# The last four heads of a two-layer decoder trunk: y loaded in place, one chain of fill work, a strictly ordered tail, and weight low parts on VectorE

## The chip, the cores and the metric

The kernel runs on one core of one Trainium2 chip. The metric is the device time in microseconds of one execution; smaller is better. Engine names in the profile are PE (TensorE, matrix products), DVE (VectorE), ACT (ScalarE), POOL (GpSimd) and SP (SyncE, which here only issues transfers). PEld is the weight load of TensorE.

## The reference

One sequence of 1024 positions and width 1024 goes through two residual layers and a final norm.

```
h = rms_norm(x, norm_g[0]);  x = x + lru_mixer(h, ...)          # layer 0: gated linear recurrence
h = rms_norm(x, norm_g[1])                                      # layer 1: forgetting attention, 16 heads of 64
u = h @ fox_w_in                                                # q, k, v, gate (1024 each) and 16 forget logits
cum = cumsum(log_sigmoid(f_logit + b_f))                        # over positions
logits = (q . k) / 8 + cum[query] - cum[key], masked causally
o = softmax(logits) @ v;   y = o * silu(gate)
x = x + y @ fox_w_out
return rms_norm(x, final_g)
```

Everything is float32. The change lies in the second layer, from its twelfth head (counted from 0) to the end: in the gate projection of the last pair of heads, in `y @ fox_w_out`, and in the final norm.

## The kernel before, in words

**Precision.** A matrix product is made of three: each float32 operand is split into a high part (rounded to the type float32r) and a low part (the rest), and high by high, low by high and high by low are accumulated in PSUM. So each weight block costs a cast on ScalarE (`to_hi`, line 75) and a subtraction (`to_lo`, line 86). `split_weights` (L88) loads a block of up to 4 x 128 columns to a tile `wf` (3 buffers), writes `wh` and `wl` (4 buffers each); `weights` (L99) does that for one column block of a weight matrix, with the subtraction on GpSimd unless `lo_eng` says otherwise. `gemm_steps` (L105) issues the three products (L111, L112, L113) for one tile of 128 x 512 and gives control back after every two blocks: one step is six products.

**The attention.** Heads come in pairs. Per head and per half c of the positions there are two streams of work: `maxima(hd, c)` (L631) makes the logits tile S of four query blocks, takes their maxima on VectorE (L659) and their exponentials on ScalarE (L662); `weigh(hd, c)` (L701) makes the transposed logits ST (L723, L724), their exponentials p (L729, L732), masks the diagonal on GpSimd (L737), splits p to `ph` and `pl` on VectorE (L81, L86), and accumulates p times v in O (L757, L758). `scale` (L696) multiplies the gate `sg` by the reciprocal sums on GpSimd (L699), `gated` (L766) multiplies the pair's result by it on GpSimd (L772) and gives y, 128 rows (a pair) by 512 positions.

**Order.** `run(order, ...)` (L786) reads a string: a digit takes a step of that stream of attention work, a dot takes a step of `fill`, other products that are to keep TensorE busy. The orders of heads 12 to 14 hold 16 dots each, the first order of head 15 holds 4, and its last two quarters of positions hold 18 and 11. A planner then puts the instructions of each engine in a fixed order, by program order and by its own estimate of when each is ready; `tc.issue_after(ins)` tells it that what the block issues on the engine of `ins` stands behind `ins` there. Each engine works through its own list strictly in order.

**What the fill is.** For an even head: `kq_units(pair + 1)` (16 steps), the next pair's keys and queries; for an odd head `g_units(pair + 1)` (8 steps), its gate. Both read `hT`, the normed input, whose 2 x 8 high and low tiles hold all 16 buffers of the tags `hh` and `hl`. In head 12 both are chained (24 steps), 16 at its dots, 8 at its end, so that `hT` is read for the last time there. From head 13 the fill is `partial` (L811, 48 steps): 16 tiles (db, c) of the output product over the first six pairs, added on VectorE to the residual x (L822), which is read from and written back to DRAM (`x1d`, L819 and L823). Its first 36 steps stand at the dots of heads 13, 14 and 15, the other 12 in the first quarter, whose last 6 dots are empty.

**y.** The y of pairs 0 to 5 goes to DRAM (`y1d`). `load_y` (L805) brings each of the 12 tiles back to a tile of the tag `xp` (3 buffers, shared with the x of `partial`), and `split_y` (L798) writes its high part on ScalarE (L75, `yhh<-y`) and its low part on VectorE (L86, `yhl<-y`) to tiles of the tags `hh` and `hl`, which come free as `hT` is no longer read. The y of pairs 6 and 7 is split directly.

**The end.** `turned(c, q)` (L827) handles a quarter of the positions: it loads the residual in four tiles (L832), and for each of two blocks b and two halves h of the width it transposes the residual onto PSUM (L850), adds the output product of pairs 6 and 7 (L854 to L856; their weights come from `late`, L883), and squares on ScalarE with a row sum (L860). For c = 0 the tile is multiplied by the norm's weight (L862) and the root is taken later for all four blocks (`root_mean`, L872; L956). For c = 1 both halves stay in PSUM until the root is known, and one VectorE instruction each (L867) multiplies by root and weight:

```
for pt, hs in zip(pts, halves):
    nc.vector.scalar_tensor_tensor(res[:, b, hs], pt, r, grow[:, hs], ALU.mult, ALU.mult)
    nc.sync.dma_start(out[4 + 2 * q + b, :, hs], res[:, b, hs])
```

The steps of `turned(0, 0)` and `turned(0, 1)` (16) are the fill of the last quarter and its rest; `turned(1, 0)` and `turned(1, 1)` follow with no order of their own.

## Time and profile before

| what | value |
|---|---|
| median of 3 runs | 1155.97 us (1154.35 to 1156.48) |
| the profiled execution | 1159.8 us |
| its span, from the first to the last instruction | 1157.9 us |
| mean granted TensorE clock of the span | 0.994 |
| PE busy | 1131.8 us (98% of the span) |
| DVE busy | 818.3 us (71%) |
| ACT busy | 590.7 us (51%) |
| POOL busy | 311.0 us (27%) |

A row of the timeline gives the start in us, the duration in us, the engine, the line of the kernel, the operation, the tile written and the tiles read, the shape, and in brackets how long the engine had been idle and what ended that. A trailing xN says that N instructions were merged in the row. A matmul's duration includes its passage through the array, and successive ones overlap; the distance between two starts is what one costs. A window's row gives for each engine the busy time in the stretch, the number of instructions, the granted TensorE clock as a share of full speed, the share of the DMA engines that were busy and the GB/s that they moved. The chain of work that ended last is followed back from the last instruction, and its pieces are shown in order of time.

### The profile page before, as it was taken

The page shows a single profiled execution, that of the slowest core. Times are in us where ns is not written, and L with a number is a line of the kernel's source. Part 1 is how long each engine was busy: PE and PEld are TensorE (multiplying, and loading weights), DVE is VectorE, ACT ScalarE, POOL GpSimd, SP SyncE. Part 2 cuts the span into 40 slices and gives each one's busy share as a digit, 9 for nine tenths or more (in the row PEclk, how much of TensorE's full clock was granted, in tenths as well). Part 3 has the DMA queues.
Part 4 walks back from the last instruction along what each step waited for, and adds up shares of the span by engine and source line. Part 5 has one row for each costly group of instructions (what it writes and reads, how often), then busy time and mean ns, then how long its engine had stood idle before and what let it go on. Part 6 is the DMA issues. An engine that isn't in the chain of part 4 may idle for free.

```text
span 1157.9 us, 15580 instructions
## 1 busy us (share of the span) xinstructions
PE 1131.8 (98%) x5565; PEld 944.8 (82%) x5565; DVE 818.3 (71%) x1294; ACT 590.7 (51%) x1009; POOL 311.0 (27%) x305
## 2 busy tenths in 40 slices
PE   9999999999999999999999999999999999999897
PEld 7787888888888887978888988889888898777685
DVE  7589766677566889556877757777577775577754
ACT  8388345345544656454554545545454454445323
POOL 1212212112021103342332333323333233141310
PEclk9999999999999999999999999999999999999898
DMA  6111111111111124351343323433234331646244
GB/s 211 51 41 50 51 51 55 42 50 41 51 59 37 55 73 151 98 142 38 92 120 92 92 64 92 120 92 83 65 92 110 92 84 60 182 138 202 80 159 182
DMA packets 60221, 105.41 MB, mean 91 GB/s; under 512 B 8744, under 2 KB 23720, under 8 KB 60144
## 3 DMA queue, kind: packets, MB, share of 16 engines
q1 hardware_dynamic: 60144, 104.42, 31.9%
q8 instruction: 44, 0.72, 0.3%
q14 instruction: 33, 0.27, 0.1%
HBM read 63.30 MB, written 15.93 MB: 68 GB/s over the span
## 4 chain that ended last, share of the span: by engine, by line
PE 47%; DVE 5%; ACT 2%; DMA 2%; issue 1%; POOL 1%; DVEq 0%; SPq 0%; ACTq 0%; POOLq 0%
PE gps L111 6%; PE gps L112 6%; PE gps L113 6%; PE O L758 3%; PE ST L723 3%; PE S L655 2%; PE S L654 2%; PE ST L724 2%; PE O L757 2%; PE vps L519 2%; PE vps L517 2%; PE vps L518 2%; DVE pl L86 2%; PE ops L112 1%; PE ops L113 1%
## 5 line engine op out<-in xcount | busy, mean ns | idle before, releaser
L86 POOL TENSOR_TENSOR wl<-wf,wh 128x512 fp32r<-128x512 f32 (+2 forms) x130 | 189.0, 1458 | 504.7 <-ACT wh L75 428.6
L111 PE MATMUL gps<-hh,wh 128*128 128x512 f32 x576 | 226.8, 394 | 1.1 <-DVE qkl L555 0.7
L113 PE MATMUL gps<-hl,wh 128*128 128x512 f32 x576 | 226.7, 394 | 0.0
L112 PE MATMUL gps<-hh,wl 128*128 128x512 f32 x576 | 226.7, 394 | 0.0
L75 ACT CAST wh<-wf 128x512 fp32r<-128x512 f32 (+2 forms) x156 | 94.0, 607 | 140.1 <-PE gps L113 43.1
L662 ACT ACTIVATE S<-S,st 128x128 f32<-128x128 f32 (+7 forms) x128 | 91.4, 714 | 114.0 <-DVE st L659 112.9
L113 PEld LDWEIGHTS gps<-hl,wh 128*128 128x128 f32 x576 | 108.3, 188 | 24.3 <-issue 0.2
L111 PEld LDWEIGHTS gps<-hh,wh 128*128 128x128 f32 x576 | 108.4, 188 | 22.6 <-DVE qkl L555 1.1
L112 PEld LDWEIGHTS gps<-hh,wl 128*128 128x128 f32 x576 | 108.5, 188 | 21.6 <-issue 0.5
L86 DVE TENSOR_TENSOR pl<-p,ph 128x512 fp32r<-128x512 f32 (+2 forms) x130 | 121.7, 953 | 2.3
L81 DVE CAST ph<-p 128x512 fp32r<-128x512 f32 (+2 forms) x130 | 79.2, 619 | 57.0 <-ACT p L729 30.2
L737 POOL TENSOR_SCALAR_AFFINE_SELECT p<-p 128x128 f32<-128x128 f32 (+1 forms) x128 | 47.5, 388 | 201.6 <-ACT p L729 98.1
L659 DVE CUSTOM_DVE_ANT_0 S<-S,mask 128x128 f32<-128x128 f32 (+7 forms) x128 | 96.6, 758 | 7.1 <-PE S L655 6.2
L351 DVE TENSOR_TENSOR x<-x,ops 128x512 f32<-128x512 f32 x80 | 54.0, 681 | 50.7 <-PE ops L113 50.6
L111 PE MATMUL ups<-hh,wh 128*128 128x512 f32 x192 | 76.3, 397 | 2.6 <-DVE us L261 1.9
L113 PE MATMUL ups<-hl,wh 128*128 128x512 f32 x192 | 75.9, 395 | 0.2
L112 PE MATMUL ups<-hh,wl 128*128 128x512 f32 x192 | 75.7, 394 | 0.3 <-POOL wl L86 0.3
L758 PE MATMUL O<-pl,v 128*128 128x512 f32 (+1 forms) x198 | 67.1, 348 | 7.8 <-DVE pl L86 7.8
L729 ACT ACTIVATE p<-ST 128x512 f32<-128x512 f32 (+1 forms) x68 | 53.0, 785 | 42.4 <-PE ST L724 35.5
L518 PE MATMUL vps<-wh,hl 128*128 128x256 f32 (+1 forms) x256 | 72.7, 285 | 0.0
L517 PE MATMUL vps<-wh,hh 128*128 128x256 f32 (+1 forms) x256 | 72.6, 285 | 0.0
L519 PE MATMUL vps<-wl,hh 128*128 128x256 f32 (+1 forms) x256 | 72.4, 284 | 0.0
(192 smaller groups left out, 2517.7 us busy)
## 6 DMA issues: line engine op xcount, KB each, us to landing
wf<-in_w SPq DMA_DIRECT2D x100, 256.0 KB
wf<-in_wo SPq DMA_DIRECT2D x64, 128.0 KB
T<-qkh SPq DMA_DIRECT2D x28, 256.0 KB
U<-qkh SPq DMA_DIRECT2D x28, 256.0 KB
x<-in_xt SPq DMA_DIRECT2D x16, 256.0 KB
x1d<-x SPq DMA_DIRECT2D x16, 256.0 KB
wf<-in_wv SPq DMA_DIRECT2D x16, 256.0 KB
xp<-x1d SPq DMA_DIRECT2D x16, 256.0 KB
```

Source lines behind the costliest of these rows:

```text
L75: nc.scalar.copy(hi, src)
L81: eng.tensor_copy(hi, src)
L86: return eng.tensor_tensor(lo, src, f32(hi), ALU.subtract)
L111: nc.tensor.matmul(o, wh, xh[:, cs], start=i == 0, stop=False)
L112: nc.tensor.matmul(o, wl, xh[:, cs], start=False, stop=False)
L113: nc.tensor.matmul(o, wh, xl[:, cs], start=False, stop=i == len(pairs) - 1)
L517: nc.tensor.matmul(pt, xh, wh, start=k == 0, stop=False)
L518: nc.tensor.matmul(pt, xl, wh, start=False, stop=False)
L519: nc.tensor.matmul(pt, xh, wl, start=False, stop=k == KT - 1)
L659: nc.vector.tensor_tensor_reduce(S[:, :n], S[:, :n], mask[:, SEQ - n :], -1.0, -NEG, ALU.add, ALU.min, accum_out=m)
L662: seen[0] = nc.scalar.activation(S[:, :n], S[:, :n], AF.Exp, bias=f32(m), scale=-1.0, accum_out=sums[:, i : i + 1])
L758: nc.tensor.matmul(o, v, pl[:, jj, : ns[jj]], start=False, stop=j == nj - 1)
```

## The change

1. `partial` asks for its weights' low parts on VectorE (`lo_eng=nc.vector`) instead of GpSimd.
2. `load_y(c)` brings the six tiles of y straight to the tiles that will hold their low parts; `split_loaded(c)` later casts the high part from there and subtracts in place. The tag `xp` is no longer used for y.
3. One chain is the fill from head 12 to the end: keys and queries of pair 7 (16 steps), the first half of its gate (4), `load_y(0)`, the second half (4), `load_y(1)`, `split_loaded(0)`, two tiles of `partial` with c = 0, `split_loaded(1)`, the other fourteen, `turned(0, 0)`, `turned(0, 1)`. It is 88 steps long; 17 are taken in head 12, 16 each in heads 13 and 14, 4 in the first order of head 15, 18 and 11 in the quarters, 6 at the end. So 7 of the gate's 8 steps go from head 12 to head 13, and no dot is empty.
4. For c = 1, each first half is multiplied by the norm's weight as soon as it is there, the second between the sum and the root; the root is then applied on ScalarE to the first half and on VectorE to the second. The residuals of c = 1 are requested ahead of the first half's output. Each step of `turned(1, 0)` and `turned(1, 1)` is put behind the last product of the step before.
5. The norm's weight (`grow`) is requested one quarter earlier, and two dots of the first quarter's order are moved by a place.

```diff
@@ -485,9 +485,8 @@
...
-        def project(cb_i, use, hs=(0, 1)):
-
-            w = list(weights(w1[cb_i]))
+        def project(w, use, hs=(0, 1)):
+
@@ -530,10 +529,11 @@
...
         kq = {}
+        wo = {}
         sgs = {}
...
         yos = {}
-        y1 = [[], []]
+        y1 = [{}, {}]
@@ -554,7 +554,7 @@
...
-                yield from project(is_k * 8 + pair, use, hs)
+                yield from project(list(weights(w1[is_k * 8 + pair])), use, hs)
@@ -615,16 +615,21 @@
...
         forget(1)
-        def g_units(pair):
-
-            sg = sgs[pair] = at.tile([P, SEQ], F32, tag="sg", name="sg1")
+        gw = [None]
+
+        def g_units(pair, hs=(0, 1)):
+
+            if hs[0] == 0:
+                sgs[pair] = at.tile([P, SEQ], F32, tag="sg", name="sg1")
+                gw[0] = list(weights(w1[16 + pair]))
+            sg = sgs[pair]
...
-            yield from project(16 + pair, use)
+            yield from project(gw[0], use, hs)
@@ -773,7 +778,7 @@
...
             if hd >= 13:
-                split_y(c, yo, nc.vector, sub)
+                split_y(c, pair, yo, sub)
             else:
@@ -795,47 +800,59 @@
...
-        def split_y(c, y, eng, sub=slice(0, HALF)):
-            if sub.start == 0:
-                y1[c].append(tuple(hpool.tile([P, HALF], F32R, tag=t, name="y" + t) for t in ("hh", "hl")))
-            yh, yl = (z[:, sub] for z in y1[c][-1])
+        def pair_of_y(c, pair):
+            y1[c][pair] = tuple(hpool.tile([P, HALF], F32R, tag=t, name="y" + t) for t in ("hh", "hl"))
+            return y1[c][pair]
+
+        def split_y(c, pair, y, sub=slice(0, HALF)):
+            yh, yl = (z[:, sub] for z in (pair_of_y(c, pair) if sub.start == 0 else y1[c][pair]))
             to_hi(yh, y, nc.scalar)
-            to_lo(yl, y, yh, eng)
-
-        def load_y(c, pairs):
-            for pair in pairs:
-                y = at.tile([P, HALF], F32, tag="xp", name="y", bufs=3)
-                nc.sync.dma_start(y, y1d[c, pair])
-                split_y(c, y, nc.vector)
-
-        def partial():
-
-
-            ws = {}
-            for db, c in [(0, 0), (1, 0), (0, 1), (1, 1)] + [(db, c) for db in range(2, KT) for c in range(2)]:
-                if db not in ws:
-                    ws[db] = list(weights(wo1[db, :, :6]))
+            to_lo(yl, y, yh, nc.vector)
+
+        def load_y(c):
+            for pair in range(6):
+                nc.sync.dma_start(f32(pair_of_y(c, pair)[1]), y1d[c, pair])
+            yield from ()
+
+        def split_loaded(c):
+            for pair in range(6):
+                yh, yl = y1[c][pair]
+                to_hi(yh, f32(yl), nc.scalar)
+                to_lo(yl, f32(yl), yh, nc.vector)
+            yield from ()
+
+        def partial(todo):
+
+
+            for db, c in todo:
+                if db not in wo:
+                    wo[db] = list(weights(wo1[db, :, :6], lo_eng=nc.vector))
                 x = at.tile([P, HALF], F32, tag="xp", name="xp", bufs=3)
...
                 pt = ps.tile([P, HALF], F32, tag="g", name="ops1")
-                yield from gemm_steps(pt, zip(ws[db], y1[c]))
+                yield from gemm_steps(pt, zip(wo[db], [y1[c][pair] for pair in range(6)]))
                 nc.vector.tensor_tensor(x, x, pt, ALU.add)
...
-        def turned(c, q):
-
-
+        left, turn = {}, [None]
+
+        def residual(c, q):
             xs = [wpool.tile([P, 2, 256], F32, tag=("wh", "wl")[q], name="x1") for d in range(4)]
...
                 nc.sync.dma_start(x, x1d[c, :, 2 * d : 2 * d + 2, q * 256 : (q + 1) * 256])
+            return xs
+
+        def turned(c, q):
+
+
+            xs = left.pop((c, q), None) or residual(c, q)
...
                 ss = ssq[c][:, 4 * q + 2 * b : 4 * q + 2 * b + 2]
-                pts = []
                 for h, hs in enumerate(halves):
@@ -843,7 +860,6 @@
...
                         pt = ps.tile([P, HALF], F32, tag="gO"[c * q], name="turn")
-                    pts.append(pt)
@@ -853,27 +869,30 @@
...
                         nc.tensor.matmul(pt, yl, wh, start=False, stop=False)
-                        nc.tensor.matmul(pt, yh, wl, start=False, stop=k == 1)
+                        turn[0] = nc.tensor.matmul(pt, yh, wl, start=False, stop=k == 1)
                         if k == 0:
...
                     nc.scalar.activation(sq, pt, AF.Square, accum_out=ss[:, h : h + 1])
-                    if c == 0:
+                    if c == 0 or h == 0:
                         nc.vector.tensor_tensor(res[:, b, hs], pt, grow[:, hs], ALU.mult)
+                        yield
+                if c == 1:
+                    r = root_mean(ss, lambda: nc.vector.tensor_tensor(res[:, b, hs], pt, grow[:, hs], ALU.mult))
+                    nc.scalar.activation(res[:, b, halves[0]], res[:, b, halves[0]], AF.Copy, scale=r)
+                    nc.vector.tensor_scalar(res[:, b, hs], res[:, b, hs], r, None, ALU.mult)
+                    for hs in halves:
+                        nc.sync.dma_start(out[4 + 2 * q + b, :, hs], res[:, b, hs])
                     yield
-                if c == 1:
-                    r = root_mean(ss)
-                    for pt, hs in zip(pts, halves):
-                        nc.vector.scalar_tensor_tensor(res[:, b, hs], pt, r, grow[:, hs], ALU.mult, ALU.mult)
-                        nc.sync.dma_start(out[4 + 2 * q + b, :, hs], res[:, b, hs])
             if c == 0:
...
-        def root_mean(ss):
+        def root_mean(ss, between=lambda: None):
...
             nc.vector.tensor_tensor(r, r, ss[:, :, 1], ALU.add)
+            between()
             nc.scalar.activation(r, r, AF.Sqrt, bias=epst, scale=1.0 / SEQ)
@@ -906,16 +925,25 @@
...
             if hd % 2 == 0:
-                if hd < 14:
+                if hd < 12:
                     fill = kq_units(pair + 1)
+                elif hd == 12:
+                    rest = [(db, c) for db in range(2, KT) for c in range(2)]
+                    fill = chain(
+                        kq_units(7),
+                        g_units(7, (0,)),
+                        load_y(0),
+                        g_units(7, (1,)),
+                        load_y(1),
+                        split_loaded(0),
+                        partial([(0, 0), (1, 0)]),
+                        split_loaded(1),
+                        partial([(0, 1), (1, 1)] + rest),
+                        turned(0, 0),
+                        turned(0, 1),
+                    )
             elif pair < 6:
                 fill = g_units(pair + 1)
-            if hd == 12:
-                fill = chain(fill, g_units(7))
-            if hd == 13:
-                load_y(0, range(3, 6))
-                load_y(1, range(6))
-                fill = partial()
             first, second = ORDERS[hd < 15 and (hd > 11 or hd % 2 == 0)]
@@ -926,12 +954,11 @@
...
             gated(hd, 1)
-            if hd == 12:
-
-                take(fill, 4)
-                load_y(0, range(3))
-            if hd < 13:
+            if hd < 12:
                 drain(fill)
+            elif hd == 12:
+
+                take(fill, 1)
             if hd % 4 == 3 and hd < 12:
@@ -939,24 +966,28 @@
...
         gated(15, 0)
-        run("0.....0...0.......0...", weigh(15, 1, quarters[0]), fill=fill)
-        drain(fill)
-        scale(15, slice(HALF, SEQ))
-        gated(15, 1, quarters[0])
         grow = at.tile([P, SEQ], F32, tag="sg", name="grow")
...
         first = []
-        fill = chain(turned(0, 0), turned(0, 1))
+        run("0.....0....0......0...", weigh(15, 1, quarters[0]), fill=fill)
+        scale(15, slice(HALF, SEQ))
+        gated(15, 1, quarters[0])
         run("0..0....0.0..0..", weigh(15, 1, quarters[1]), fill=fill)
...
+
+        for q in range(2):
+            left[1, q] = residual(1, q)
         r = root_mean(ssq[0])
...
             nc.sync.dma_start(out[i], o)
-        for q in range(2):
-            drain(turned(1, q))
+        tail = chain(turned(1, 0), turned(1, 1))
+        while turn[0] is not None:
+            with tc.issue_after(turn[0].ins):
+                if next(tail, tail) is tail:
+                    break
```

## The prediction, made before the changed kernel was run

> **What bounds the kernel now.** I read the page's busy shares first, then the stretch from head 12 to the end cut at the places where TensorE pauses, then who TensorE waited for.
>
> ```profile
> PE 1131.8 (98%) x5565; PEld 944.8 (82%) x5565; DVE 818.3 (71%) x1294; ACT 590.7 (51%) x1009; POOL 311.0 (27%) x305
> core 0: us, PE busy (x) PEld busy (x) DVE busy (x) ACT busy (x) POOL busy (x), PEclk, DMA share, GB/s
> 975.00:1020.00 45.00, 42.55 (x193) 34.19 (x192) 28.24 (x49) 20.41 (x38) 7.13 (x12) 1.00 0.54 147
> 1020.00:1070.00 50.00, 49.47 (x234) 40.35 (x233) 36.04 (x69) 24.27 (x50) 15.21 (x18) 1.00 0.58 171
> 1070.00:1084.00 14.00, 10.17 (x37) 8.06 (x37) 11.88 (x13) 4.10 (x9) 7.01 (x9) 0.76 0.31 98
> 1084.00:1113.70 29.70, 29.64 (x149) 24.69 (x148) 18.15 (x31) 9.16 (x17) 8.54 (x11) 1.00 0.36 116
> 1113.70:1137.50 23.80, 23.40 (x141) 20.00 (x140) 11.86 (x22) 9.10 (x25) 2.11 (x4) 1.00 0.46 143
> 1137.50:1157.90 20.40, 11.76 (x60) 8.88 (x58) 9.68 (x21) 7.42 (x22) 0.00 (x0) 0.83 0.54 207
> PE O L758 <- DVE pl L86: 5.1, 2, 3.8
> PE turn L850 <- ACT sq L860: 2.5, 1, 2.5
> PE ST L723 <- ACT S L662: 1.6, 2, 1.2
> PE turn L850 <- DMA x<-x1d: 0.4, 1, 0.4
> ```
>
> TensorE sets the time: it is busy for 98% of the span, and the change takes no product away and adds none. So it can only win back time in which TensorE pauses or runs at less than full clock. Subtracting the busy column from each stretch gives the pauses: 2.45 us before 1020, 0.53 to 1070, 3.83 in the 14 us after it, 0.06, 0.40, and 8.64 at the end. The last four rows (wait in us, how often, the longest) name them: two waits for `pl`, one for a square, two for an exponential, one for the residual's transfer. The row 1070 to 1084 shows a second loss, a clock of 0.76. The next rows show that place on three engines (DVE, POOL, PE), and two rows from a quiet place for comparison.
>
> ```profile
> 1069.56 7.00 DVE L86 TENSOR_TENSOR pl<-p,ph 128x1024 fp32r<-128x1024 f32 x1
> 1069.46 2.39 POOL L699 TENSOR_TENSOR sg<-sg,recb 64x1024 f32<-64x1024 f32 x1 [14.22 <-DMA recb<-recd]
> 1071.80 0.55 POOL L737 TENSOR_SCALAR_AFFINE_SELECT p<-p 128x128 f32<-128x128 f32 x2
> 1072.30 3.18 POOL L86 TENSOR_TENSOR wl<-wf,wh 128x512 fp32r<-128x512 f32 x3
> 1076.62 0.80 PE L758 MATMUL O<-pl,v 128*128 128x512 f32 x1 [3.83 <-DVE pl L86]
> 1077.21 0.63 PE L757 MATMUL O<-ph,v 128*128 128x512 f32 x1
> ...
> 1082.33 0.50 PE L113 MATMUL ops<-yhl,wh 128*128 128x512 f32 x1
> 1005.48 0.39 PE L112 MATMUL ops<-yhh,wl 128*128 128x512 f32 x1
> 1005.71 0.40 PE L113 MATMUL ops<-yhl,wh 128*128 128x512 f32 x1
> 1066.60 1.22 DVE L86 TENSOR_TENSOR pl<-p,ph 128x1024 fp32r<-128x1024 f32 x1
> ```
>
> The subtraction that gives `pl` takes 7.00 us where the same one just before took 1.22. During it GpSimd ran without a break for 2.39 + 0.55 + 3.18, and VectorE's instruction ended about one us after GpSimd's last. I read it as VectorE standing still while GpSimd works. The Trainium skill, page "SBUF — State Buffer", section "Who interferes with whom", gives the reason: a VectorE instruction with two SBUF inputs shares a read path with GpSimd, and whoever starts first holds it for the whole instruction; the rows agree. After 3.83 us of idleness TensorE comes back slow: from 1077.21 to 1082.33 there are twelve distances between starts, 5.12 / 12 = 0.43 us each, against 0.23 at 1005.48. That is 12 x 0.20 = 2.4 us. This place costs 3.83 + 2.4 = 6.2 us.
>
> **Low parts on VectorE.** 8 weight tiles with two pieces each, 16 subtractions, leave GpSimd for VectorE. Their rows between 995 and 1115 (14 of 16), VectorE's price for the same two shapes (here of y), and what stays on GpSimd:
>
> ```profile
> L86 POOL TENSOR_TENSOR wl<-wf,wh 128x512 fp32r<-128x512 f32 x7 | 9.2, 1315 | 16.8 <-ACT wh L75 16.5 <-POOL sg L699 0.4
> L86 POOL TENSOR_TENSOR wl<-wf,wh 128x256 fp32r<-128x256 f32 x7 | 6.2, 885 | 12.3 <-ACT wh L75 12.0 <-DMA xp<-x1d 0.2
> L86 DVE TENSOR_TENSOR yhl<-y,yhh 128x512 fp32r<-128x512 f32 x12 | 8.0, 687 | 8.2 <-ACT yhh L75 7.9 <-PE gps L112 0.3
> L86 DVE TENSOR_TENSOR yhl<-yo,yhh 128x256 fp32r<-128x256 f32 x2 | 0.8, 416 | 0.0
> L772 POOL TENSOR_TENSOR yo<-yo,sg 128x512 f32<-128x512 f32 x3 | 4.1, 1370 | 7.0 <-DVE yo L763 7.0
> ```
>
> VectorE gets 8 x 0.687 + 8 x 0.416 = 8.8 us more. Its rows from 975 to 1113.7 add up to 28.24 + 36.04 + 11.88 + 18.15 = 94.3 of 138.7 us, 68%; with 8.8 more 74%. The sum is covered by TensorE's own work, the queue is not: behind each subtraction stand VectorE's casts and subtractions for `ph` and `pl`, which TensorE awaits at O, and the subtraction itself waits for ScalarE's cast, which waits for the weight's transfer. GpSimd loses 8 x 1.315 + 8 x 0.885 = 17.6 us and with it most of its power to hold VectorE up. At 1069.56, 3.18 of GpSimd's 6.1 us go away, so `pl` comes 3.18 earlier, TensorE idles 0.65 us, and I take it that the clock then stays up, as it did in the rows of 975 to 1020 with a wait of 1.2: gain 3.18 + 2.4 = 5.6. Bounds: 6.2 if the rest closes too; nothing, if VectorE is by then so late that the pause returns. The new load costs 0 where it falls into the free 26%, and at most two waits like the one of 1.2, 2.4; I take 1.0, nearer to the free share. The other side of the skill's rule speaks against the edit: the moved subtractions have two SBUF inputs, so GpSimd's remaining 2.39 and 1.37 us instructions can hold them up as well; by it one or two in 16 would last about a us longer, which the 1.0 contains.
>
> **y in place.** The 12 transfers, 12 casts and 12 subtractions all stay. They no longer pass through the three buffers `xp`, but their room is free only once TensorE has read `hT` for the last time, half by half.
>
> ```profile
> L75 ACT CAST yhh<-y 128x512 fp32r<-128x512 f32 x12 | 7.2, 619 | 8.9 <-DMA y<-y1d 8.9
> 992.81 8.69 SPq L808 DMA_DIRECT2D y<-y1d  x6
> ```
>
> Now ScalarE waits 8.9 us in all for these transfers, six of which take SP 8.69 us because each waits for a buffer; the transfers of weights stand behind them in SP's queue. With 7 of the gate's 8 steps moved into head 13, four steps of fill (24 products at 0.23, 5.5 us) plus attention work stand between `load_y` and its use, and the same for the second half: I cost the transfers at nothing, hidden by those steps; were they not, TensorE would wait about one transfer queue, 8.69 less 5.5, some 3. But six casts and six subtractions now come in one piece: 6 x 0.619 = 3.7 us on ScalarE and 6 x 0.687 = 4.1 on VectorE, with exponentials and `pl` behind them. The wait of 1.2 for an exponential and the smaller one for `pl` (5.1 - 3.8 = 1.3) are of that kind already. I take back 1.0 of the 2.45; bounds a gain of 2.45 and a loss of 3.
>
> **The strict tail.**
>
> ```profile
> 1146.87 2.43 ACT sq L860 x8
> 1149.35 0.65 PE L850 MATMUL turn<-ident,x 128*128 128x128 f32 x4 [2.51 <-ACT sq L860]
> 1150.94 0.41 PE turn L855
> 1151.35 0.44 PE turn L856
> 1152.53 0.17 DVE ssq L876
> 1153.05 0.18 DVE ssq L878
> 1153.32 1.41 DVE L867 SCALAR_TENSOR_TENSOR res<-turn,ssq,grow 128x512 f32<-128x512 f32 x2
> 1139.28 2.74 DVE L956 TENSOR_SCALAR res<-res,ssq 128x1024 f32<-128x1024 f32 x4
> ```
>
> The planner mixed the tiles of c = 1: four were squared in one go, and the last tile waited 2.51 us for a bank. The eight tiles of c = 1 have eight banks by their tags (two each of g and O, two pairs of S), so in strict order no tile has to wait for another of its kind: 2.5 gained. Bounds: 2.9, with the slow clock of the last two products (0.41 and 0.44 against 0.23), and 1.0, if strict order makes TensorE wait for a residual or for a bank of c = 0. After the last square the old way was sum, root, inverse, 1.41: 2.2 us from 1152.53 to 1154.73. The new one is sum 0.17, product 0.7, inverse 0.18, then ScalarE's scaling (a cast of that size took 0.62) beside VectorE's (2.74 / 8 = 0.34): about 1.8 with hand-overs, but the first half's transfer, until now 0.7 us ahead of the second's, starts later than before. I take 0; bounds a gain of 0.4 and a loss of 0.4.
>
> **One chain.** TensorE's sum is unchanged and no step is lost. But `partial` now ends one dot into the last quarter, and `turned(0, 0)` needs its last buffers and its last residual.
>
> ```profile
> 1113.84 0.24 PE ops L112
> 1114.60 4.49 DMA x<-x1d
> 1119.14 0.44 PE turn L850 x2
> ```
>
> From the chain of waits: the residual took 4.49 us after the last product of `partial`, covered until now by the last quarter's attention; TensorE lost only the 0.40 seen above. One of that quarter's four pairs of key blocks (8 products of half the width, half of 0.23 each, 0.9 us) may now stand ahead of it, so I take a loss of 0.7; bounds 0 and 2.7 (4.49 less a first tile of `turned`, whose residual is there: 0.44 for the transposes and six products at 0.23, 1.8).
>
> **Sum.** -5.6 + 1.0 - 1.0 - 2.5 + 0.7 = -7.4 us. The profiled execution took 1159.8 (span 1157.9, the other 1.9 outside it), so it would take 1152.4. It lies 3.8 above the median of 1155.97; I carry the gain over: 1148.6.
>
> **The rivals.** *VectorE's queue becomes the bound (slower).* A moved subtraction waits at the head of VectorE's queue for a weight that is late, `pl` waits behind it, and TensorE pauses long enough to lose its clock. For it: the idle columns above show that GpSimd sat 16.5 and 12.0 us for ScalarE's cast, a wait that VectorE inherits where it gets there early. Against: ScalarE's queue stands still in the same wait already. Price: 6.2 per case, the place at 1069. It decides from the second case on: -7.4 + 2 x 6.2 = +5.0, 1161. Chance 0.13.
>
> *The pause returns elsewhere.* TensorE's pauses in heads 13 to 15 stay as long as before, since the planner does not know that GpSimd holds VectorE and its new order makes a new collision; only the tail's 2.5 holds, less 0.7 and 1.0: 1155.2. For it: 2.39 us of GpSimd's scaling remain at each head. Against: only one of these pauses was over 1.3 us. Chance 0.19. By the Trainium skill ("TensorE: Matmul & The Clock Gate", "HAM oscillation — how this bites in real kernels") an idle time of about 3.4 us costs the clock; here 3.83 did and 1.2 did not, which agrees.
>
> *All pauses go.* 3.83 + 2.4 + 2.45 + 0.53 + 2.9 = 12.1: 1143.9. For it: the fill has no empty dots. Against: the bursts of casts. Chance 0.10.
>
> *The forecast*, between 1145 and 1153: 0.58.
>
> **The numbers.** A measurement of this kernel tells about 0.2%, 2.3 us, from no change. Below 1153.7 lie the forecast, the last rival and a third of the second: 0.58 + 0.10 + 0.06 = 0.74, less 0.02 for the forecast's upper edge, 0.72. Within 2.3 us lie the rest of the second and that edge, 0.15; above, 0.13. The range leaves out the slower rival (0.13) and the best few cases: 1143.5 to 1157.5.
>
> **What would show it.** In the changed profile no `wl` on GpSimd from head 13 on; no `pl` above 4.5 us; the clock 1.00 from 975 to 1137; the largest wait of TensorE before the tail under 2 us; no wait of a transpose for a square; the span's last product 2 to 3 us nearer to the one that ends `partial`. Wrong: a wait of TensorE over 3 us followed by a clock below 0.9, a VectorE row for `wl` that stands idle for ScalarE's cast with `pl` behind it, or casts of y that wait for transfers.

## The result and the profile after: slower by 0.9%

The changed kernel takes 1166.31 us (median, 1165.29 to 1167.63); the kernel before took 1156.11 beside it. The ratio is 1.0089, with a 95% interval of 1.0076 to 1.0103. The forecast was 1148.6 and a range up to 1157.5. The profiled execution of the changed kernel took 1165.29 (span 1163.6).

First the page's busy row, then the stretch from head 12 to the end cut where TensorE pauses now (columns as in the prediction), then who TensorE waited for there.

```profile
PE 1134.5 (98%) x5565; PEld 946.6 (81%) x5565; DVE 826.0 (71%) x1314; ACT 593.7 (51%) x1013; POOL 293.6 (25%) x289
```

```profile
975.00:1000.00 25.00, 25.00 (x119) 20.89 (x118) 14.96 (x27) 9.64 (x18) 2.05 (x6) 1.00 0.56 145
1000.00:1030.00 30.00, 24.58 (x95) 18.21 (x94) 26.46 (x50) 18.30 (x37) 6.31 (x8) 0.83 0.51 135
1030.00:1062.00 32.00, 32.00 (x151) 26.55 (x150) 20.52 (x41) 12.34 (x26) 2.86 (x5) 1.00 0.42 140
1062.00:1070.00 8.00, 5.25 (x17) 3.95 (x16) 5.10 (x7) 4.25 (x7) 3.08 (x3) 0.79 0.56 170
1070.00:1113.00 43.00, 43.00 (x215) 36.13 (x214) 30.19 (x55) 13.70 (x28) 7.72 (x12) 1.00 0.40 126
1113.00:1142.00 29.00, 28.86 (x162) 24.06 (x161) 13.33 (x24) 10.90 (x28) 1.84 (x3) 1.00 0.48 154
1142.00:1163.60 21.60, 11.18 (x57) 8.32 (x56) 9.98 (x24) 8.36 (x22) 0.00 (x0) 0.96 0.51 195
```

```profile
PE turn L866 <- DVE res L878: 4.5, 2, 2.6
PE ST L728 <- ACT p L734: 3.1, 2, 2.7
PE O L763 <- DVE pl L86: 2.6, 3, 0.9
PE S L659 <- ACT S L667: 1.3, 1, 1.3
```

TensorE runs without a gap from 975 to 1000, 1030 to 1062 and 1070 to 1113. It loses at three places: 1000 to 1030 (5.42 us idle and a clock of 0.83), 1062 to 1070 (2.75 idle, 0.79), and the tail.

To put one number on a stretch I add up, over its products, by how much the distance to the next start exceeds the distance at full speed (0.23 us for 512 columns, 0.12 for 256, as the rows of quiet places show). This counts idle time and slow products alike, and the span less all such losses is about 1117 us in the kernel before (1157.9 - 40.6) and after (1163.6 - 46.6; 40.6 and 46.6 are the sums of their rows), so losses account for the difference. In us, by trace:

| kernel | to 975 | place 1, 1000-1035 | place 2, 1040-1085 | 1085-1125 | tail, from 1125 | span |
|---|---|---|---|---|---|---|
| before | 22.5 | 3.4 | 8.3 | 1.4 | 5.0 | 1157.9 |
| before, second profile (e4) | 23.4 | 2.8 | 4.0 | 1.9 | 5.7 | 1155.0 |
| after | 21.9 | 11.9 | 4.7 | 0.6 | 7.5 | 1163.6 |
| e2: after, two tiles in the tail | 21.6 | 11.1 | 3.8 | 1.5 | 2.5 | 1157.4 |
| e3: before, low parts on VectorE | 21.7 | 2.4 | 1.6 | 1.5 | 5.3 | 1149.6 |
| e7: e3, strict order, two tiles | 24.5 | 3.2 | 1.5 | 1.6 | 1.8 | 1149.6 |
| e8: e2, y through `xp` | 23.0 | 9.7 | 7.1 | 0.2 | 3.2 | 1162.2 |
| e9: e2, gate in head 12 | 22.7 | 7.5 | 1.5 | 2.2 | 2.0 | 1152.8 |
| e11: e9, a late piece moved | 21.6 | 3.1 | 0.6 | 3.0 | 1.5 | 1146.7 |
| e13: e9, y through `xp` | 22.7 | 3.5 | 1.5 | 2.5 | 1.7 | 1148.7 |

Each row is one execution. Up to 975, where the edits do not reach, the rows differ by up to 2.9 us; the profile of e9 is the slowest of its ten runs (1154.62), that of e11 the fastest of its ten (1148.42); e8 loses about 2 us more between 1035 and 1040, outside the columns.

So place 2 loses 3.6 us less than in the profile that the prediction used, but 0.7 more than in the second one, while place 1 loses 8.5 and the tail 2.5 more. Place 1, read on five engines (timeline of the changed kernel):

```profile
992.53 4.89 SPq L814 DMA_DIRECT2D yhl<-y1d  x5
1004.28 0.39 PE L113 MATMUL gps<-hl,wh 128*128 128x512 f32 x1
1012.73 0.47 SPq L695 DMA_DIRECT2D recb<-recd  x1
1016.25 2.60 POOL L704 TENSOR_TENSOR sg<-sg,recb 64x1024 f32<-64x1024 f32 x1 [1.24 <-DMA recb<-recd]
1019.52 1.28 POOL L777 TENSOR_TENSOR yo<-yo,sg 128x512 f32<-128x512 f32 x1
1020.84 0.62 ACT L75 CAST yhh<-yo 128x512 fp32r<-128x512 f32 x1 [2.63 <-POOL yo L777]
1021.36 3.22 ACT L75 CAST yhh<-yhl 128x512 fp32r<-128x512 f32 x6
1022.87 0.63 PE L111 MATMUL ops<-yhh,wh 128*128 128x512 f32 x1
```

The last product of the gate starts at 1004.28 and the first of `ops` at 1022.87: for 18.6 us TensorE has no fill at all, only attention work with its short waits (the `pl` and S rows above). The y transfers of the first half were issued by 997.4. Their six casts run only at 1021.36, directly behind the cast of `yo`, which is the split of pair 6 and waits for the whole chain of that head's sums: `recb`, GpSimd's scaling 2.60, its gating 1.28. On ScalarE's list the six casts stand behind that split. The second half's transfers were issued only from 1021.26 to 1025.9, and their casts waited 0.99 and 0.46 us for them (at 1027.93 and 1029.01).

Place 2 and the tail in the same timeline:

```profile
1055.62 1.65 ACT L75 CAST woh<-wf 128x512 fp32r<-128x512 f32 x3
1064.21 0.62 ACT L75 CAST woh<-wf 128x512 fp32r<-128x512 f32 x1 [6.94 <-DMA wf<-in_wo]
1064.74 1.94 ACT L734 ACTIVATE p<-ST 128x1024 f32<-128x1024 f32 x2
1065.81 0.50 PE L728 MATMUL ST<-U,T 128*128 128x512 f32 x1 [2.75 <-ACT p L734]
1141.48 2.74 DVE L984 TENSOR_SCALAR res<-res,ssq 128x1024 f32<-128x1024 f32 x4
1146.15 0.66 PE L866 MATMUL turn<-ident,x 128*128 128x128 f32 x4 [2.65 <-DVE res L878]
1155.59 0.66 PE L866 MATMUL turn<-ident,x 128*128 128x128 f32 x4 [1.83 <-DVE res L878]
```

At place 2 a late weight's cast stands in ScalarE's queue 6.94 us for its transfer, two exponentials stand behind it, and TensorE waits 2.75 for them. In the tail the second half of block b = 1 waits twice for the reader of its first half. Both halves lie in one tile, `two_banks`.

### The profile page after: what moved, and what is told of

It is laid out like the page before. It is cut to its first block, busy times and chain, and to the rows that moved or that the text cites. A ratio compares the mean times of both kernels' runs of the same rounds, so it can differ in the third digit from the quotient of the medians.

```text
span 1163.6 us, 15563 instructions
## 1 busy us (share of the span) xinstructions
PE 1134.5 (98%) x5565; PEld 946.6 (81%) x5565; DVE 826.0 (71%) x1314; ACT 593.7 (51%) x1013; POOL 293.6 (25%) x289
## 4 chain that ended last, share of the span: by engine, by line
PE 49%; DVE 5%; DMA 2%; ACT 2%; issue 1%; POOL 0%; SPq 0%; ACTq 0%; DVEq 0%; POOLq 0%
PE gps L111 7%; PE gps L113 7%; PE gps L112 7%; PE S L660 3%; PE S L659 3%; PE ST L728 3%; PE O L763 3%; PE O L762 3%; PE ST L729 2%; PE vps L518 2%; PE vps L516 2%; PE vps L517 2%; PE ops L113 2%; PE ops L111 1%; PE ops L112 1%
## 5 line engine op out<-in xcount | busy, mean ns | idle before, releaser
L86 POOL TENSOR_TENSOR wl<-wf,wh 128x512 fp32r<-128x512 f32 (+1 forms) x114 | 172.4, 1518 | 471.4 <-ACT wh L75 396.4
L112 PEld LDWEIGHTS gps<-hh,wl 128*128 128x128 f32 x576 | 108.5, 188 | 21.9 <-POOL wl L86 0.6
L111 PEld LDWEIGHTS gps<-hh,wh 128*128 128x128 f32 x576 | 108.4, 188 | 21.9 <-DVE qkl L555 1.1
L86 DVE TENSOR_TENSOR pl<-p,ph 128x512 fp32r<-128x512 f32 (+2 forms) x130 | 116.9, 916 | 2.3
```

What stands on the lines that cost most here:

```text
L86: return eng.tensor_tensor(lo, src, f32(hi), ALU.subtract)
L111: nc.tensor.matmul(o, wh, xh[:, cs], start=i == 0, stop=False)
L112: nc.tensor.matmul(o, wl, xh[:, cs], start=False, stop=False)
```

## The experiments

"sep" in a name means that the two halves of that block have a tile of one bank each. The kernel before, run beside each set, had medians of 1155.2 (e1 to e4), 1155.78 (e5 to e8 and e9 to e12) and 1155.27 (e13 to e15); ratios are to it.

**e1, e2: one cause each, taken out of the changed kernel.** e1 puts the split of pair 6's first half behind the second run of head 13; e2 gives the halves a tile each:

```
e1  -            if hd >= 13:
    +            if hd == 13 and c == 0:
    +                later.append((c, pair, yo, sub))     # split after run(second, ...)
    +            elif hd >= 13:
e2  -                        if h == 0:
    -                            two = two_banks("turn")
    -                        pt = two[:, h]
    +                        pt = ps.tile([P, HALF], F32, tag="S", name="turn")
```

> The changed kernel, but the split of pair 6's first half (a cast and a subtraction that wait for head 13's reciprocals and two GpSimd instructions) is traced after the casts of the loaded y instead of before them. Theory A (the planner gives the buffers of one tag out in program order, so the twelve casts of y stand behind that late cast on ScalarE, and TensorE has no fill from 1005 to 1023): the casts start near 1000, the stretch 1005 to 1030 loses under 3 us instead of about 12, and the time falls by 6 to 9 us to some 1157 to 1160. Theory B (the burst of twelve casts and subtractions itself, or VectorE's new subtractions, make the pauses): under 2 us of change, 1164 to 1167.

> The changed kernel, but the two halves of block b = 1 of the tail stand in two PSUM tiles instead of in one tile of two banks. Theory A (the second half's transposes wait for the readers of the first half because both are one tile): the waits of 2.65 and 1.83 us of a transpose for the product with the norm's weight go, and the time falls by 3 to 5 us to some 1161 to 1163. Theory B (they wait because VectorE is late with the scaling of the first half of the output, whatever the tile): the waits stay, 1165 to 1167.

e1: 1164.08 (ratio 1.0071, 1.0056 to 1.0086). The casts did move, to 993.62, so it was the split of pair 6 that held them; but by the medians only 2.2 us came of it, and the interval overlaps that of the changed kernel (1.0076 to 1.0103). In its profile place 1 loses about 5 us less than in the changed kernel, each of the other stretches up to about 1 more, and the span is 1.8 shorter (1161.8). What is left at place 1:

```profile
993.62 0.62 ACT L75 CAST yhh<-yhl 128x512 fp32r<-128x512 f32 x1 [2.73 <-DMA yhl<-y1d]
1003.81 0.50 PE L659 MATMUL S<-T,U 128*128 128x512 f32 x1 [1.20 <-ACT p L737]
1007.39 0.58 PE L728 MATMUL ST<-U,T 128*128 128x256 f32 x1 [1.88 <-ACT S L667]
1008.42 0.63 PE L111 MATMUL gps<-hh,wh 128*128 128x512 f32 x1
1012.26 0.63 PE L111 MATMUL ops<-yhh,wh 128*128 128x512 f32 x1
```

The twelve casts now come with head 13's exponentials behind them. TensorE waits 1.20 and 1.88, and ten starts from 1008.42 to 1012.26 lie 0.43 apart (3.84 / 9). e2: 1159.08 (1.0040, 1.0026 to 1.0054), by the medians 7.2 us faster than the changed kernel, more than the 3 to 5 expected. The tail's loss falls from 7.5 to 2.5 and no transpose waits for `res`: shown. Place 1 stays, at 11.1.

**e3, e4: the low parts alone, and the kernel before once more.** e3 is the kernel before with `lo_eng=nc.vector` in `partial`; e4 changes nothing.

> The kernel before with one edit of the change alone: the low parts of partial's weights on VectorE. Theory A (GpSimd's hold on VectorE at the pause of 3.83 us was real and typical): 4 to 6 us faster than before, 1150 to 1152. Theory B (that pause with its slow clock was a property of the one profiled execution, 3.8 us above the median): 0 to 2.5 us faster, 1153.5 to 1156. Theory C (VectorE's queue becomes the bound): slower by over 2 us.

> The kernel before once more, unchanged, for a second profile. Theory B of the run before: its time lies near 1156, the span near 1154, and the pause near 1072 is under 3 us or is not followed by a slow clock. Theory A: the pause of 3.8 us and 12 slow products are there again, span near 1158.

e3: 1151.37 (0.9968, 0.9956 to 0.9980), 3.8 us faster. e4 (one run, 1157.05) shows the pause on which the prediction had built its largest term, as another execution has it:

```profile
1069.85 3.45 DVE L86 TENSOR_TENSOR pl<-p,ph 128x1024 fp32r<-128x1024 f32 x1
1073.36 0.50 PE L758 MATMUL O<-pl,v 128*128 128x512 f32 x1 [0.28 <-DVE pl L86]
1073.82 3.10 DVE L680 TENSOR_SCALAR sums<-sums 128x4 f32<-128x4 f32 x1
1074.99 0.50 PE L112 MATMUL ops<-yhh,wl 128*128 128x512 f32 x1 [0.67 <-POOL wl L86]
```

The same `pl` took 3.45 rather than 7.00, TensorE waited 0.28, and there were no slow products. The 6.2 us were of one execution; place 2 cost 4.0 here. What the prediction read as VectorE standing still beside GpSimd is there too, on another instruction: L680, four columns, took 3.10 us while GpSimd made three `wl` (1073.67 to 1076.89), and 0.15 in the first profile, where it came after them. And TensorE waited 0.67 for a `wl` of GpSimd itself, which the prediction had not counted (in e5 it waited 1.36).

**e5, e6, e7: the strict order, on the kernel before.** e5 has the strict order alone; e6 is e3 with two tiles in the old order; e7 is e6 in strict order.

> The kernel before, with the second half of the output issued in strict order and nothing else changed. Theory (two halves of one tile): the wait of 2.5 us for a square comes from the two halves of block b = 1 lying in one two-bank tile of PSUM, so that the second half's transposes wait for the first half's reader; strict order does not take that away, it makes the wait come twice, each about as long as a square and its hand-over (1 to 2 us). So 1155 to 1158, with two waits of a transpose for a square. Rival (the order was at fault, as the prediction had it): no wait of a transpose over 0.5 us and 1152.5 to 1154.

> The kernel before, with the low parts of the last weights on VectorE and the two halves of block b = 1 in two tiles of PSUM of one bank each. If the two effects are independent and add: 1151.4 - 2.5 = 1149, and no wait of a transpose for a square. If a bank of its own only moves the wait (to a residual, or to the tile before): 1151 to 1152.

> The same as the run before it in this set, with the second half of the output in strict order as well. With banks of their own the planner's mixed order has nothing to wait for either, so strict order should change under 1 us: 1148 to 1150. If strict order by itself costs (a transpose waits for the residual or for the banks of the first half of the output), 1151 or more. Beside the changed kernel with separate banks (1159.1) this one lacks only y in place, the one chain and the new arithmetic at the end, so the difference is their joint price: 8 to 11 us if the theory of the late casts holds, 3 or less if not.

e5: 1155.76 (0.9999, 0.9984 to 1.0015); e6: 1156.03 (0.9995, 0.9981 to 1.0009), where e3 had 0.9968; e7: 1149.42 (0.9938, 0.9914 to 0.9962). Their waits in the tail, of e5 and then of e6 (us in total, times, longest):

```profile
PE turn L852 <- ACT sq L862: 2.5, 2, 1.8
```

```profile
PE turn L848 <- DVE res L865: 4.9, 1, 4.9
```

e5 is as the first theory had it: strict order splits the one wait of 2.5 into two that add up to 2.5. e6 refuted my expectation: a tile of its own in the planner's order is worse, because tiles are begun ahead and the next one then waits 4.9 us for a multiplication out of an earlier tile, which stands behind that tile's root. Only both together help: from e6 to e7 strict order gives 0.6% (I had expected under 1 us). From e3 to e7 it is 0.3% by the ratios, whose intervals still touch; in the profiles the tail's loss falls from 5.3 to 1.8, and no transpose waits for an engine. e7 lies 9.7 us under e2, inside the 8 to 11 expected if the late casts are what costs. So strict order was right only with tiles of one bank.

**e8, e9, e13: how y comes in, and where the gate stands.** All three are e2 with one or two edits:

```
e8  load_y:  + y = at.tile(..., tag="xp"); dma_start(y, y1d[c, pair]); split_y(c, pair, y)
             (split_loaded left empty)
e9  -                take(fill, 1)
    +                take(fill, 8)
e13 both
```

> The changed kernel with separate banks (1159.1), and y loaded through the three buffers xp and split on arrival, as in the kernel before; the one chain of fill stays. Theory (the late casts come from splitting later: their tiles are handed out behind the split of pair 6): the casts start before 1010 us and the stall of TensorE at 1004 to 1023 goes, so 5 to 9 us faster: 1150 to 1154. Rival (the one chain is at fault: it puts the whole gate of pair 7 ahead, and leaves no fill for head 13's start however y comes in): 1157 to 1161, with a stall of over 5 us at the same place.

> The changed kernel with separate banks (1159.1), and the whole gate of pair 7 again issued at the end of head 12, as in the kernel before; y stays in place and is split as before in this kernel. Theory (one chain: the fill behind the gate now starts inside head 13, so the split of y comes behind pair 6's split and head 13 has no fill): the casts of y move ahead of pair 6's split, the stall of TensorE at 1004 to 1023 shrinks to the 2 to 3.5 us of the kernel before: 1149 to 1152. Rival (y in place is at fault, wherever the gate stands, since six casts and subtractions come in one piece): a stall of over 6 us remains there, 1155 or more.

> The changed kernel with separate banks, the whole gate of pair 7 at the end of head 12, and y loaded through the buffers xp and split on arrival. Against the run with the gate first and y in place (1153.8) only y's way in differs. If y in place has a price of its own (the second half's six casts wait for their transfers at the head of ScalarE's queue, with the first exponentials of the next block behind them: 4.4 us waited there in that run): 1149 to 1151, as the kernel before with low parts, strict order and separate banks (1149.4), and a wait of ST for that exponential of 2.2 us or less. If not: 1152.5 to 1155.

e8: 1163.93 (1.0057, 1.0033 to 1.0082). This is above both ranges. The first half's casts did move, to 990.13, and TensorE has fill from 1006.85 to 1019.25; but then it has none until 1037.42, 18.2 us, about as long as before. The stall came later and did not go, so splitting later was not at fault by itself. Place 1 still costs 9.7, and about 2 more up to 1040, now because the second half's casts stand behind the same split (and the next one, at 1028.82, waits 3.21 for its transfer):

```profile
1022.26 0.62 ACT L75 CAST yhh<-yo 128x512 fp32r<-128x512 f32 x1 [2.89 <-POOL yo L777]
1022.79 1.66 ACT L75 CAST yhh<-y 128x512 fp32r<-128x512 f32 x3
```

e9: 1153.80 (0.9971, 0.9956 to 0.9985). With the gate's eight steps issued in head 12 again, as before, the kernel is by the medians 5.3 us faster than e2, and faster than the kernel before. The casts begin at 993.53, ahead of pair 6's split, and place 2 falls to 1.5 without being touched, since exponentials now stand ahead of the late cast (first two rows). What is left at place 1 is the next three:

```profile
1067.95 1.94 ACT L734 ACTIVATE p<-ST 128x1024 f32<-128x1024 f32 x2
1072.63 0.62 ACT L75 CAST woh<-wf 128x512 fp32r<-128x512 f32 x1 [2.74 <-DMA wf<-in_wo]
1006.90 1.30 ACT L75 CAST yhh<-yhl 128x512 fp32r<-128x512 f32 x2 [2.03 <-DMA yhl<-y1d]
1010.45 0.77 ACT L667 ACTIVATE S<-S,st 128x640 f32<-128x640 f32 x1
1011.38 0.79 PE L728 MATMUL ST<-U,T 128*128 128x512 f32 x1 [4.42 <-ACT S L667]
```

A cast of the second half waits 2.03 for its transfer, an exponential comes after it, and TensorE waits 4.42. This is the slowest run of e9: in the profile of e11, with the same code there, the wait is 2.2 and place 1 loses 3.1. e13: 1151.62 (0.9971, 0.9956 to 0.9985), with a wait of 2.4 there. The medians differ by 2.2 us in favour of `xp`, the ratios not at all, and e9's runs reach from 1148.18 to 1154.62: a price of y in place by itself is not shown. With the gate inside head 13 the medians speak for it (e2 1159.08, e8 1163.93), but the intervals of the ratios overlap: not shown either.

**e10, e11, e14, e15: place 2.** e10 (on e2) and e11 (on e9) issue the fourth piece of the late weights in head 15; e14 (on e2) and e15 (on e7) let GpSimd issue the transfers `recd` and `recb` of heads 13 to 15, so that SP's queue does not stand in their wait:

```
e10, e11  - run(second, ..., side=side); drain(side)
          + run(second, ..., side=itertools.islice(side, 3))   # the rest: run(first, ..., side=side) of head 15
e14, e15  - nc.sync.dma_start(recd..., rc[:nb]) and the one of recb
          + (nc.gpsimd if hd >= 13 else nc.sync).dma_start(...)
```

> The changed kernel with separate banks (1159.1), and only the fourth piece of the late weights (one of four loads, casts and subtractions) issued in head 15 rather than at the end of head 14. Theory (second stall: that cast stands on ScalarE ahead of two exponentials and waits for its transfer): the stall of 2.8 to 3.7 us at 1061 to 1066 goes, 1155 to 1156.5. Rival (TensorE waits there for something else that only ends at about the same time): 1158 to 1160, with a wait of an ST product of over 1.5 us.

> Both edits of the two runs before it. If the three causes found so far (one tile for two halves, the gate inside head 13, the fourth late piece) are all there is: 1146 to 1149, under every kernel so far. If the late piece costs nothing once the gate is ahead (the planner then puts the exponentials first by itself): as the run with the gate alone, 1149 to 1152.

> The changed kernel with separate banks (1159.1), and for heads 13 to 15 the two transfers of the inverse sums (recd, recb) issued by GpSimd, not SP, so that the loads of weights no longer stand behind SP's wait for them. If the second stall is made by that queue: the weights' loads land 2 to 3 us earlier, ScalarE's wait of 5 to 7 us for wf at 1055 to 1064 shrinks by as much and TensorE's stall at 1061 to 1066 (2.8 to 3.7 us with the slow products) goes: 1155 to 1157. If the loads wait for their three buffers and not for SP: the stall stays, 1158.5 to 1161.

> The kernel before with low parts on VectorE, strict order and separate banks (1149.4), and the same two transfers issued by GpSimd. That kernel's largest wait there is one of 2.0 us at 1007, which has no such transfer ahead, and none over 0.6 us at 1060 to 1080: no change over 1 us, 1148.5 to 1150.5. If SP's wait costs wherever it stands: 1146 to 1148.

e10: 1162.57 (1.0057, 1.0042 to 1.0072); e14: 1160.66 (1.0057, 1.0042 to 1.0072). e10 misses both its ranges, e14 lies in that of its rival; neither is faster than e2. Their timelines, e10's first:

```profile
1066.24 0.92 ACT L75 CAST wh<-wf 128x512 fp32r<-128x512 f32 x2 [5.76 <-DMA wf<-in_wo]
1068.14 0.50 PE L728 MATMUL ST<-U,T 128*128 128x512 f32 x1 [1.87 <-ACT p L734]
```

```profile
1058.19 0.81 SPq L908 DMA_DIRECT2D wf<-in_wo  x2
1064.48 0.62 ACT L75 CAST woh<-wf 128x512 fp32r<-128x512 f32 x1 [6.00 <-DMA wf<-in_wo]
```

In e10 another weight's cast takes the place of the moved one. In e14 the load is issued at 1058.19, 1.4 us after ScalarE begins the three casts ahead of it (1056.83); in e2 it was 3.3 us after (1057.84, 1054.52). So SP's wait did hold the load up, by some 2 us, but nothing came of it: from issue to cast it now takes 6.3 us, in e2 3.6, and TensorE waits 1.83 for the exponential, in e2 1.12. Meanwhile the DMA engines are 0.75 and then 0.89 busy in e14 (1058 to 1061, 1061 to 1064), 0.81 in e2 (1058 to 1061). What makes the place, as I read it, is ScalarE's order, a cast whose weight is still under way ahead of exponentials; why the transfer takes that long stays open. e11: 1153.00 (0.9970, 0.9956 to 0.9983) is not told from e9; e15: 1149.64 (0.9961, 0.9947 to 0.9976) not from e7.

**e12: the low parts inside the changed kernel.** e2 with `wl` back on GpSimd.

> The changed kernel with separate banks (1159.1), and the low parts of the last weights back on GpSimd. If the edit is worth inside the changed kernel what it was alone (3.8 us): 1162 to 1164. If the fill's shortage hides it or the added load on VectorE is what makes the burst at 1021 long: 1155 to 1159.5.

1164.21 (1.0069, 1.0054 to 1.0084), against 1.0040 for e2: some 0.3% or 3.4 us, as alone. This part of the change works in both settings.

The best kernel is e7: the kernel before with low parts on VectorE, strict order and a tile for each half, 1149.42, 0.62% under the kernel before (interval 0.38 to 0.86) and by the medians 1.4% under the changed one (1149.42 / 1166.31).

## Why the prediction was wrong, point by point

**Low parts on VectorE (-5.6 and +1.0).** The mechanism held in the main: in e3 TensorE waits 0.2 us in all for `pl`, in the two profiles of the kernel before 5.1 and 0.8. What else the edit saves, TensorE's waits for `wl` itself, is not separated from it. GpSimd issues no `wl` after head 12, and VectorE does them in 10.1 us where I had 8.8 (rows of the changed kernel between 975 and 1140, by shape):

```profile
L86 DVE TENSOR_TENSOR wl<-wf,wh 128x512 fp32r<-128x512 f32 x8 | 5.5, 687 | 1.4 <-ACT wh L75 1.2
L86 DVE TENSOR_TENSOR wl<-wf,wh 128x256 fp32r<-128x256 f32 x8 | 4.6, 573 | 1.3 <-ACT wh L75 1.3
```

The size was off: -3.8 in all (e3) for -4.6. The 5.6 was read from one execution, 3.8 us above its median, and e4's pause was shorter.

**The strict tail (-2.5).** Wrong in its sign. The step that failed is "The eight tiles of c = 1 have eight banks by their tags (two each of g and O, two pairs of S), so in strict order no tile has to wait for another of its kind". The pairs of S are single tiles of two banks, and the second half's products wait for the first half's reader. I counted banks where the wait goes by tile. Worse, the reader is now VectorE's multiplication by `grow`, which the first time stands behind the four scalings of the first half of the output (2.74 us at 1141.48): two waits, 4.5, for one of 2.5. With strict order and the old arithmetic (e5) the two waits added up to 2.5, so the other 2.0 go with the new arithmetic, which no run tests by itself. Separate tiles alone give the changed kernel 0.5% (1.0089 to 1.0040 in e2), and strict order helps once they are there (e6 to e7).

**The end of the tail (0).** Right: from the last sum to the span's end 5.2 us (1158.41 to 1163.6) against 5.4 (1152.53 to 1157.9).

**y in place (-1.0) and one chain (+0.7).** Here lies about half of the error of 17.7 us (1166.31 for 1148.6): 8.5 us at place 1 (11.9 for 3.4). The step that failed is "TensorE's sum is unchanged and no step is lost. But `partial` now ends one dot into the last quarter": it prices the chain where it ends, and puts the start of head 13, which loses its fill, at nothing without a reason. Beside it stands "I cost the transfers at nothing, hidden by those steps". The first half's were hidden indeed (issued by 997.4, 24 us before their use), the second half's nearly (0.99 and 0.46 of waits on ScalarE), and my bound of "some 3" was for late transfers. What I had not asked is what else the later place moves. The chain starts `partial` inside head 13, so the casts come behind pair 6's split on ScalarE; the gate's steps are used up at 1004 and TensorE has no fill until 1022.87. The price at its end was in the bounds (0.7; in e9 and e13 a transpose waited 1.3 us for its residual there, in the changed kernel none did). Putting the gate back gives 5.3 us by medians and 0.7% by the ratios of e2 and e9. With the tail's tiles and the gate both put right the ratio goes from 1.0089 to 0.9971; the forecast was 0.9936 (1148.6 / 1155.97). Why the casts stand behind that split I only argued: both write tiles of one tag, which are handed out in the order of the program. e1 and e9 show that with another order in the program they move ahead.

**The rivals.** The slower rival has the right sign and, by chance, nearly the size (1161), but not the mechanism: no subtraction of a late weight held `pl` up; the `wl` rows stood only 1.4 and 1.3 us idle in all. "The pause returns elsewhere" is half right: a new order made a new collision, mainly on ScalarE. GpSimd has a small part: beside its scaling at 1016.25 a `pl` of 512 columns took 2.15 us, and TensorE waited 0.89 for it.

**What was to show it.** No `wl` on GpSimd, and no `pl` over 4.5: right. The clock of 1.00 up to 1137 (0.83 and 0.79 at two places), no wait over 2 us (2.75): wrong. No transpose waits for a square, as said, but two wait for the multiplication instead. The last product was to come 2 to 3 us nearer to the one that ends `partial`: it stands 1.0 us farther (1119.05 to 1157.26, before 1113.91 to 1151.15). The third sign against the forecast, casts of y that wait, came true, mainly for a neighbour's gating and only by 0.99 and 0.46 us for transfers.

## What to carry to other kernels

When fill work is moved to a later place, ask not only whether its inputs are there, but what now stands ahead of it in each in-order queue, and until when the old place goes without fill. Count dependences by tile, not by bank: two halves in one tile wait for each other's readers. And before a gain is sized by one pause of one profile, look at a second execution.

## What the runs showed of the hardware

The clock fell after shorter pauses than I had taken it to need. In the prediction 3.83 us cost it and 1.2 did not. In the changed kernel the wait of 2.75 at 1065.81 was followed by products 0.43 apart, and in e1 waits of 1.20 and 1.88, 3.6 us apart, were as well; in e13 a single wait of 2.36 was not. Nor does the length of a wait settle it: in the changed kernel one of 1.27 at 1007.43 was followed by products 0.43 apart, in e2 the same wait, also of 1.27, by products 0.23 apart (1008.33 to 1008.56). What decides between the two is not shown here.

```profile
1067.41 0.63 PE L659 MATMUL S<-T,U 128*128 128x512 f32 x1
1067.84 0.63 PE L660 MATMUL S<-T,U 96*128 96x512 f32 x1
```

```profile
1007.43 0.44 PE L659 MATMUL S<-T,U 128*128 128x384 f32 x1 [1.27 <-ACT S L667]
1009.25 0.63 PE L728 MATMUL ST<-U,T 128*128 128x512 f32 x1
1009.67 0.63 PE L729 MATMUL ST<-U,T 128*128 128x512 f32 x1
```

```profile
1007.15 0.45 PE L659 MATMUL S<-T,U 128*128 128x384 f32 x1 [1.27 <-ACT S L667]
```

```profile
1009.33 0.51 PE L728 MATMUL ST<-U,T 128*128 128x512 f32 x1 [2.36 <-ACT S L667]
1010.26 0.39 PE L111 MATMUL ops<-yhh,wh 128*128 128x512 f32 x1
1010.49 0.40 PE L112 MATMUL ops<-yhh,wl 128*128 128x512 f32 x1
```

The first two blocks are the changed kernel's timeline (0.43 between starts), the third e2's, the last e13's (0.23). The Trainium skill ("TensorE: Matmul & The Clock Gate", "HAM oscillation — how this bites in real kernels") gives pauses over about 3.4 us as the rule; the measurement here differs, 2.75 and once 1.27 was enough. And one subtraction started beside the same GpSimd scaling took 7.00 us in one execution and 3.45 in another. In the first GpSimd ended its three `wl` (1075.48) before it, in the second it ended (1073.30) before the first `wl` began (1073.67). That its length goes by how much of GpSimd's next work catches it is my reading of these two, not tested.
